# Query and key rows of a differential attention, split once over all 128 partitions

## The chip, the core and the metric

The kernel runs on one core of a Trainium2 chip. TensorE (PE) multiplies, VectorE (DVE) and ScalarE (ACT) read its results in PSUM and prepare operands in SBUF, GpSimd (POOL) does small work, and SyncE (SP) issues nearly all DMAs from one queue. Each engine runs its own queue in order. The metric is device time of one execution in microseconds (us), as the median of several runs; less is better.

## The reference

One layer: an RMS norm, one input projection, then two groups of heads side by side (differential attention, and a gated delta rule with a scan over chunks), an output projection, and an MLP with a squared ReLU. Everything is float32. The part that the change touches is the attention of group A, four heads with two softmax maps each:

```python
da_q = rms_norm(da_q.reshape(B, S, DA_HEADS, 2, DA_QK_DIM), q_norm_w[l])   # S = 1024, heads 4, dim 64
da_k = rms_norm(da_k.reshape(B, S, DA_HEADS, 2, DA_QK_DIM), k_norm_w[l])
...
s = jnp.einsum('bqhcd,bkhcd->bhcqk', qb, k) * scale
s = jnp.where(causal, s, jnp.finfo(jnp.float32).min)
p = jax.nn.softmax(s, axis=-1)
a = p[:, :, 0] - lam * p[:, :, 1]
out = jnp.einsum('bhqk,bkhe->bqhe', a, v)
```

## The kernel before

Float32 accuracy is made of products of rounded parts: an operand x becomes xH (rounded to the format that PE multiplies fast, `F32R`) and xL = x - xH. A large product is then three matmuls, H by H, H by L and L by H.

The work goes in stages. First come the projection of gates and of the delta rule's inputs (0 to about 250 us), then a stage in which many streams share PE (about 250 to 620 us), then the MLP. In the middle stage a planner, the class `Interleave`, writes PE's order: each stream is a generator that yields the time from which it can go on. The planner keeps its own clock `now`, which PE work advances (`flow.pe`). The streams have priorities: `scan` (the delta rule), `horner`, `mixed`, `da_turns`, `values`, `scores`, `da_units` and `outproj`. With `flow.chain` a stream estimates when a series of ACT and DVE instructions will be done, and with `flow.hold` how long a PSUM bank stays taken. The estimates are `act(n)` = 55 + 0.83 n ns and `vec(n, extra)` = 68 + 1.045 n + extra ns; `chain` adds a quarter of the series' length as margin (`MARGIN`). A store may be put off to a planned time (`flow.put_off`). PE's order is fixed this way; the order on ACT, DVE, POOL and SP is left to the framework's scheduler.

The streams around the change:

- `da_units` (L987) projects queries, keys and values in three units of 512 columns, eight blocks of 128 tokens each (matmuls L1012 to L1014, in two PSUM banks `pj`). Its weights come in pieces `wraw` (L211), which ACT rounds to `wH` (L213) and DVE subtracts to `wL` (L214).
- `leave` (L1028) empties a bank: ACT scales it to `qn` (L1040, or L1034 and L1035), POOL and DVE norm it. It queues the normed pieces of 256 columns (two heads of queries or of keys) in the list `late` and doesn't start while more than two stand there.
- `da_turns` (L957) takes each of the 32 pieces: PE transposes it into `ps_qkt` (L965, L966), so that a partition holds one of 2 x 64 components (m is the softmax map, 64 partitions each) and the columns are 2 heads x 128 tokens. ACT and DVE split it into a tile `qa` (L972, L973, two buffers), which goes to `qk_d` in DRAM (L977).
- `scores` (L1094) loads the keys of a head into `KS0` and `KS1`, one for each map (`load_head`, L1068), and for each block of 128 queries `qa` and `qb` (`load_q`, L1085 to L1087), one block ahead. A score is two matmuls over 128 partitions, `qa` by `KS` (L1148) and `qb` by `KS` (L1149): with H and L parts stacked in the two halves of the partitions, one gives HH + LL and the other LH + HL.
- `values` (L1175) transposes the weights of the softmax (L1189) and multiplies by the values (L1201); `outproj` (L1279) multiplies with the output weights (L1291 to L1293).

Before, `qa` was stored with the halves already in the place where the matmul wants them: for map 0 the H part in partitions 0 to 63 and L in 64 to 127, for map 1 the other way round. So a split took two ACT and two DVE instructions over 64 partitions each, DVE writing to the other half than it read. A key tile was loaded with one DMA, `qa` with one, and `qb`, its halves swapped, with two.

Of the kernel before, what the change touches and what calls it, by code (L numbers as in the profile page):

```python
# [9 lines left out]
F32 = mybir.dt.float32  # L10
F32R = mybir.dt.float32r
BF16 = mybir.dt.bfloat16
AF = mybir.ActivationFunctionType
ALU = mybir.AluOpType
# [4 lines left out]
P = 128  # L19
# [100 lines left out]
def act(n, accum=False):  # L120
    return "S", 55.0 + 0.83 * n + (93.0 if accum else 0.0)


def vec(n, extra=0.0):
    return "V", 68.0 + 1.045 * n + extra
# [7 lines left out]
def tile_hymba_layer(  # L133
# [6 lines left out]
    nc = tc.nc  # L140
    V, S, G, T = nc.vector, nc.scalar, nc.gpsimd, nc.tensor
# [49 lines left out]
    qk_d = dram.tile([2, 2, NT, P, 2, 2, P], F32, name="qk_d")  # L191
# [264 lines left out]
    for tb in range(NT):  # L456
        T.matmul(tail[:, 300 + 2 * tb:302 + 2 * tb], ssum_[:, tb * P:(tb + 1) * P], ones[:, 0:2],
                 start=True, stop=True)
# [305 lines left out]
    flow = Interleave()  # L764
# [3 lines left out]
    HF = (slice(0, 64), slice(64, 128))  # L768
# [186 lines left out]
    late, accs, vts, v_at, qa_free = [], {}, {}, {}, [0.0] * 3  # L955

    def da_turns():  # L957
        for i in range(4 * NT):
            while not late:
                yield flow.now + 50, None  # L960
            g, kind, tb, qn, t = late[0]
            r = yield from flow.bank("px", at=max(t + 2000, qa_free[i % 2] - 500))
            late.pop(0)
            pt = px.tile([P, 512], F32, tag="px", name="ps_qkt")
            T.transpose(pt[:, 0:P], qn[:, 0:P], ident)  # L965
            T.transpose(pt[:, P:2 * P], qn[:, P:2 * P], ident)  # L966
            flow.begun(("qa", i % 2))
            qa = sd.tile([P, 2, 256], F32R, tag="qa", name="qa", bufs=2)
            wv = qw if kind == 0 else kw
            for m in range(2):  # L970
                a, b = HF[m], HF[1 - m]
                S.activation(qa[a, m, :], pt[a, 0:256], AF.Copy, scale=wv[a])  # L972
                V.scalar_tensor_tensor(qa[b, m, :], pt[a, 0:256], wv[a], qa[a, m, :].bitcast(F32),  # L973
                                       ALU.mult, ALU.subtract)
            flow.pe(2 * TR)
            t = flow.chain(act(256), act(256), vec(256, 60), vec(256, 60), start=max(flow.now, qa_free[i % 2]))
            flow.put_off(t, ("qa", i % 2), lambda g=g, kind=kind, tb=tb, qa=qa: nc.sync.dma_start(  # L977
                qk_d[g, kind, tb], qa.bitcast(F32).rearrange("p m (h t) -> p m h t", h=2)))
            qa_free[i % 2] = t + DMA_T
            flow.hold(r, t)  # L980
            state["turned"] += 1
            if state["turned"] % (2 * NT) == 0:
                flow.due(lambda t, key: key[0] == "qa")
                state["da"] += 1
                state["da_t"] = flow.now + 6000
        sdctx.close()
# [77 lines left out]
    def load_head(h, pool):  # L1064
        KS = []
        for m in range(2):
            k = pool.tile([P, SEQ], F32R, tag=f"KS{m}", name=f"KS{m}")
            nc.sync.dma_start(k.bitcast(F32).rearrange("p (b t) -> p b t", t=P),  # L1068
                              qk_d[h // 2, 1, :, :, m, h % 2, :].rearrange("b p t -> p b t"))
            KS.append(k)  # L1070
        return KS

# [8 lines left out]
    def load_q(h, tb):  # L1081
        qa = ap.tile([P, 2, P], F32R, tag="qa", name="qa", bufs=2)
        qb = ap.tile([P, 2, P], F32R, tag="qb", name="qb", bufs=2)
        src = qk_d[h // 2, 0, tb, :, :, h % 2, :]
        nc.sync.dma_start(qa.bitcast(F32), src)  # L1085
        nc.sync.dma_start(qb[HF[0]].bitcast(F32), src[HF[1]])
        nc.sync.dma_start(qb[HF[1]].bitcast(F32), src[HF[0]])  # L1087
        return qa, qb

    order = [(0, t) for t in range(NT)] + [(1, t) for t in range(NT)]  # L1090
# [3 lines left out]
    def scores():  # L1094
        heads, loaded, npe, nsc, since = {}, {}, 0, 0, 0
        while state["da"] < 1:
            yield flow.now + 300, None
        heads[0] = load_head(0, ap), load_v(0, ap)
        q = load_q(*order[0])
        yield state["da_t"] + 3000, None  # L1100
        for u, (h, tb) in enumerate(order):
            if h == 1 and h not in heads:
                while not (state["scan"] and len(v_at) == NT):
                    yield flow.now + 300, None
                heads[1] = load_head(1, pools["a2"]), load_v(1, pools["a2"])
                loaded[1] = flow.now + 9000
            if h > 0 and state["da"] > 1 and 2 not in heads:
                heads[2] = load_head(2, ap), load_v(2, ap)
                loaded[2] = max(flow.now, state["da_t"]) + 4000
# [8 lines left out]
            if q is None and h > 0:  # L1118
                q = load_q(h, tb)
# [3 lines left out]
            if q is None:  # L1123
                q = load_q(h, tb)
                yield flow.now + 3000, None
# [381 lines left out]
    flow.add(2, values())  # L1507
    flow.add(3, scores())
    flow.add(1.6, da_turns())
    flow.add(4, da_units())  # L1510
    flow.add(1.4, mix_loads())
# [343 lines left out]
```

## Time and profile before

| | us |
|---|---|
| median of 3 runs | 1226.38 (1225.47 to 1226.53) |
| the profiled execution | 1226.58 |
| its span, first to last instruction | 1224.9 |
| PE busy in the span | 1212.0 |
| DVE busy | 850.0 |
| ACT busy | 604.6 |
| POOL busy | 121.0 |

The span is one execution under the profiler. Lines such as L972 are those of the listing above. A group of instructions is named by line, engine and operation, then output <- inputs, shapes and count. A wait is put down to whatever released it. PE is busy for almost the whole span, and its matmuls overlap in the records, so a busy share of 99% says only that there are few gaps. The granted clock is the share of its full speed at which PE was allowed to run.

### The profile page before, as it was taken

The page shows a single profiled execution, that of the slowest core. Times are in us where ns is not written, and L with a number is a line of the kernel's source. Part 1 is how long each engine was busy: PE and PEld are TensorE (multiplying, and loading weights), DVE is VectorE, ACT ScalarE, POOL GpSimd, SP SyncE. Part 2 cuts the span into 40 slices and gives each one's busy share as a digit, 9 for nine tenths or more (in the row PEclk, how much of TensorE's full clock was granted, in tenths as well). Part 3 has the DMA queues.
Part 4 walks back from the last instruction along what each step waited for, and adds up shares of the span by engine and source line. Part 5 has one row for each costly group of instructions (what it writes and reads, how often), then busy time and mean ns, then how long its engine had stood idle before and what let it go on. Part 6 is the DMA issues. An engine that isn't in the chain of part 4 may idle for free.

```text
span 1224.9 us, 17632 instructions
## 1 busy us (share of the span) xinstructions
PE 1212.0 (99%) x6330; PEld 1029.2 (84%) x6330; DVE 850.0 (69%) x1448; ACT 604.6 (49%) x1176; POOL 121.0 (10%) x162
## 2 busy tenths in 40 slices
PE   9999999999999999999999999999999999999998
PEld 9988888898888888888788888888888888888887
DVE  7786788477868577766798554566577955786553
ACT  8565545234556555656666444454554333333331
POOL 0011110223332230212100000000000000000000
PEclk9999999999999999999999999999999999999999
DMA  6564442456755584434528433443279855433301
GB/s 230 176 182 125 112 130 87 116 183 218 241 161 180 173 244 135 115 80 142 183 86 291 155 127 133 170 174 135 103 253 353 325 185 183 160 104 104 138 35 69
DMA packets 161087, 199.04 MB, mean 163 GB/s; under 512 B 21008, under 2 KB 120936, under 8 KB 161000
## 3 DMA queue, kind: packets, MB, share of 16 engines
q1 hardware_dynamic: 160856, 197.79, 49.3%
q8 instruction: 50, 0.82, 0.3%
q14 instruction: 37, 0.30, 0.1%
q10 hardware_dynamic: 144, 0.13, 0.0%
HBM read 132.32 MB, written 65.56 MB: 162 GB/s over the span
## 4 chain that ended last, share of the span: by engine, by line
PE 89%; DVE 4%; DMA 3%; ACT 2%; issue 1%; SPq 0%; POOL 0%; ACTq 0%; DVEq 0%
PE X L1454 5%; PE X L1453 5%; PE X L1452 5%; PE X L1768 4%; PE X L1769 4%; PE X L1770 4%; PE ps_dn L221 4%; PE ps_dn L219 4%; PE ps_dn L220 4%; PE ps_qk L1012 3%; PE Y L1454 3%; PE Y L1453 3%; PE Y L1452 3%; PE ps_qk L1014 3%; PE ps_qk L1013 2%; PE ps_o L1201 2%
## 5 line engine op out<-in xcount | busy, mean ns | idle before, releaser
L1371 ACT CAST hH<-ur 128x1024 fp32r<-128x1024 f32 x56 | 58.6, 1048 | 166.0 <-PE X L1769 79.7
L1372 DVE TENSOR_TENSOR hL<-ur,hH 128x1024 fp32r<-128x1024 f32 x56 | 68.5, 1224 | 79.8 <-ACT hH L1371 79.8
L1372 DVE TENSOR_TENSOR op<-raw,op 128x1024 fp32r<-128x1024 f32 x48 | 58.7, 1223 | 75.3 <-PE X L1453 42.3
L1768 PE MATMUL X<-hH 128*128 128x512 f32 x224 | 87.2, 389 | 0.0
L1769 PE MATMUL X<-hL,hH 128*128 128x512 f32 x224 | 87.2, 389 | 0.0
L1770 PE MATMUL X<-hH,hL 128*128 128x512 f32 x224 | 87.2, 389 | 0.0
L1012 PE MATMUL ps_qk<-wH,hH 128*128 128x512 f32 x192 | 82.2, 428 | 1.9 <-ACT qn L1040 1.9
L1014 PE MATMUL ps_qk<-wH,hL 128*128 128x512 f32 x192 | 75.8, 395 | 0.0
L219 PE MATMUL ps_dn<-hH,wH 128*128 128x512 f32 x192 | 75.7, 394 | 0.0
L220 PE MATMUL ps_dn<-hL,wH 128*128 128x512 f32 x192 | 75.6, 394 | 0.0
L1013 PE MATMUL ps_qk<-wL,hH 128*128 128x512 f32 x192 | 75.4, 393 | 0.1
L221 PE MATMUL ps_dn<-hH,wL 128*128 128x512 f32 x192 | 75.4, 393 | 0.0
L1372 DVE TENSOR_TENSOR hL<-dw,hH 128x1024 fp32r<-128x1024 f32 x56 | 68.2, 1220 | 3.2 <-ACT hH L1371 3.2
L1371 ACT CAST op<-raw 128x1024 fp32r<-128x1024 f32 x48 | 50.4, 1050 | 34.8 <-PE Y L1454 20.1
L1371 ACT CAST hH<-dw 128x1024 fp32r<-128x1024 f32 x56 | 58.6, 1047 | 16.7 <-DMA dw<-in_w_down_dram 5.1
L1157 ACT ACTIVATE pexp<-ps_sc,mx 128x128 f32<-128x128 f32 (+7 forms) x64 | 47.3, 740 | 26.1 <-DVE mx L1153 26.1
L595 DVE SCALAR_TENSOR_TENSOR cy<-cp,pv,cy 128x512 f32<-128x512 f32 x72 | 53.7, 750 | 7.8 <-ACT cy L593 7.0
L1153 DVE TENSOR_REDUCE mx<-ps_sc 128x1 f32<-128x128 f32 (+7 forms) x64 | 47.5, 754 | 14.1 <-PE ps_sc L1151 13.5
L1291 PE MATMUL ps_op<-wH,hH 128*128 128x512 f32 x128 | 53.6, 419 | 0.0
L1293 PE MATMUL ps_op<-wH,hL 128*128 128x512 f32 x128 | 50.3, 393 | 0.0
L1292 PE MATMUL ps_op<-wL,hH 128*128 128x512 f32 x128 | 50.0, 391 | 0.0
L1453 PE MATMUL Y<-hL,op 128*128 128x512 f32 x128 | 49.8, 389 | 0.0
(355 smaller groups left out, 3383.8 us busy)
## 6 DMA issues: line engine op xcount, KB each, us to landing
ur<-ud SPq DMA_DIRECT2D x28, 1024.0 KB, 4.9
raw<-in_w_up_dram SPq DMA_DIRECT2D x32, 512.0 KB, 3.7
dw<-in_w_down_dram SPq DMA_DIRECT2D x32, 512.0 KB, 7.2
qk_d<-qa SPq DMA_DIRECT2D x32, 256.0 KB, 3.1
ud<-ua SPq DMA_DIRECT2D x16, 512.0 KB, 4.0
ud<-s SPq DMA_DIRECT2D x16, 512.0 KB, 3.2
wraw<-in_w_in_dram SPq DMA_DIRECT2D x24, 256.0 KB, 3.5
wraw<-in_w_in_dram SPq DMA_DIRECT2D x48, 128.0 KB, 2.9
```

Of the source, the lines that this page charges most:

```text
L219: T.matmul(ps, lh(k), rh(k), start=(k == 0), stop=False)
L220: T.matmul(ps, lh(k), rl(k), start=False, stop=False)
L221: T.matmul(ps, ll(k), rh(k), start=False, stop=(k == n - 1))
L1012: T.matmul(ps, hH[:, 4 * kh + k, sl], wh[:, k, :], start=(kh + k == 0), stop=False)
L1013: T.matmul(ps, hH[:, 4 * kh + k, sl], wl[:, k, :], start=False, stop=False)
L1014: T.matmul(ps, hL[:, 4 * kh + k, sl], wh[:, k, :], start=False, stop=(kh + k == 4))
L1371: S.copy(dst[0], src)
L1372: V.tensor_tensor(dst[1], src, dst[0].bitcast(F32), ALU.subtract)
L1453: T.matmul(ps, op[0][:, k, cs], h[1][:, k, :], start=False, stop=False, skip_group_check=True)
L1768: T.matmul(o, v[0][:, j, sl], v[2][:, j, c], start=s0, stop=False, skip_group_check=True)
L1769: T.matmul(o, v[0][:, j, sl], v[3][:, j, c], start=False, stop=False, skip_group_check=True)
L1770: T.matmul(o, v[1][:, j, sl], v[2][:, j, c], start=False, stop=s1, skip_group_check=True)
```

## The change

A turned piece is split once over all 128 partitions: `qa[:, 0]` takes the H part and `qa[:, 1]` the L part of both maps, and the tile is stored as it lies. The halves are brought to their places when they are loaded: each key tile with two DMAs of 64 partitions, `qa` with two and `qb` with two. The planner's estimate for a piece changes with it, from two ACT and two DVE instructions to one of each.

```diff
-            for m in range(2):
-                a, b = HF[m], HF[1 - m]
-                S.activation(qa[a, m, :], pt[a, 0:256], AF.Copy, scale=wv[a])
-                V.scalar_tensor_tensor(qa[b, m, :], pt[a, 0:256], wv[a], qa[a, m, :].bitcast(F32),
-                                       ALU.mult, ALU.subtract)
+            S.activation(qa[:, 0, :], pt[:, 0:256], AF.Copy, scale=wv)
+            V.scalar_tensor_tensor(qa[:, 1, :], pt[:, 0:256], wv, qa[:, 0, :].bitcast(F32), ALU.mult, ALU.subtract)
             flow.pe(2 * TR)
-            t = flow.chain(act(256), act(256), vec(256, 60), vec(256, 60), start=max(flow.now, qa_free[i % 2]))
+            t = flow.chain(act(256), vec(256, 60), start=max(flow.now, qa_free[i % 2]))
             flow.put_off(t, ("qa", i % 2), lambda g=g, kind=kind, tb=tb, qa=qa: nc.sync.dma_start(
-                qk_d[g, kind, tb], qa.bitcast(F32).rearrange("p m (h t) -> p m h t", h=2)))
+                qk_d[g, kind, tb], qa.bitcast(F32).rearrange("p x (h t) -> p x h t", h=2)))
...
             k = pool.tile([P, SEQ], F32R, tag=f"KS{m}", name=f"KS{m}")
-            nc.sync.dma_start(k.bitcast(F32).rearrange("p (b t) -> p b t", t=P),
-                              qk_d[h // 2, 1, :, :, m, h % 2, :].rearrange("b p t -> p b t"))
+            kv = k.bitcast(F32).rearrange("p (b t) -> p b t", t=P)
+            for x in range(2):
+                nc.sync.dma_start(kv[HF[x]], qk_d[h // 2, 1, :, HF[m], x, h % 2, :].rearrange("b p t -> p b t"))
...
-        src = qk_d[h // 2, 0, tb, :, :, h % 2, :]
-        nc.sync.dma_start(qa.bitcast(F32), src)
-        nc.sync.dma_start(qb[HF[0]].bitcast(F32), src[HF[1]])
-        nc.sync.dma_start(qb[HF[1]].bitcast(F32), src[HF[0]])
+        parts = [qk_d[h // 2, 0, tb, :, x, h % 2, :].rearrange("(m r) t -> r m t", m=2) for x in range(2)]
+        for t, swap in ((qa, 0), (qb, 1)):
+            for x in range(2):
+                nc.sync.dma_start(t[HF[x]].bitcast(F32), parts[x ^ swap])
         return qa, qb
```

## The prediction

> **What bounds the kernel now.** I read the page first, then the busy time by stage, then what TensorE (PE) waited for, then the instructions around its longest wait, and last the chain that leads into that wait.
>
> ```profile
> span 1224.9 us, 17632 instructions
> PE 1212.0 (99%) x6330; PEld 1029.2 (84%) x6330; DVE 850.0 (69%) x1448; ACT 604.6 (49%) x1176; POOL 121.0 (10%) x162
> ...
> 260.00:300.00 40.00, 40.00 (x253) 35.49 (x252) 35.04 (x95) 18.94 (x51) 15.26 (x16) 1.00 0.68 216
> 300.00:335.00 35.00, 33.07 (x192) 28.59 (x191) 28.98 (x76) 15.67 (x42) 10.69 (x11) 0.95 0.75 235
> 335.00:400.00 65.00, 63.82 (x349) 53.77 (x348) 47.01 (x117) 41.97 (x113) 18.14 (x24) 1.00 0.58 177
> 400.00:460.00 60.00, 58.62 (x324) 50.22 (x322) 39.25 (x96) 34.39 (x85) 18.90 (x23) 1.00 0.70 210
> ```
>
> The first two rows are the page; the others are stretches of the span (length, then busy time of PE, PE's weight loads, DVE, ACT, POOL, then the granted PE clock, DMA share and GB/s). PE is idle for 1224.9 - 1212.0 = 12.9 us of the whole run, so a change that leaves PE's own instructions alone can win no more than that, plus time in which PE runs at a lower clock. The changed lines run between 261 and 455 us. There DVE is the second bound: 35.04 of 40 us at 260 to 300. The row to see is 300 to 335: PE loses 1.93 us and its clock is 0.95.
>
> The waits of PE from 250 to 575 us are these, all of them:
>
> ```profile
> PE ps_qk L1012 <- ACT qn L1040: 1.9, 1, 1.9
> PE ps_sc L1148 <- ACT pexp L1157: 1.4, 2, 0.9
> PE ps_at L1189 <- DVE pexp L1167: 1.0, 1, 1.0
> PE ps_at L1189 <- DVE hL L260: 0.6, 2, 0.4
> PE ps_at L1189 <- ACT om L1207: 0.6, 1, 0.6
> ```
>
> One wait of 1.9 us stands out: the projection (L1012) wants a PSUM bank that ACT has not yet emptied (L1040). PE's own order of time around it, and three stretches of 4 us:
>
> ```profile
> 306.49 0.39 PE L1014 MATMUL ps_qk<-wH,hL 128*128 128x512 f32 x1
> 308.79 0.50 PE L1012 MATMUL ps_qk<-wH,hH 128*128 128x512 f32 x1 [1.91 <-ACT qn L1040]
> ...
> 310.39 0.63 PE L1014 MATMUL ps_qk<-wH,hL 128*128 128x512 f32 x1
> ...
> 308.00:312.00 4.00, 3.21 (x12) 2.79 (x13) 3.84 (x9) 3.59 (x11) 2.23 (x2) 0.71 0.56 170
> 312.00:316.00 4.00, 4.00 (x21) 3.45 (x21) 3.93 (x13) 2.16 (x4) 2.45 (x3) 0.87 0.76 231
> ...
> 340.00:344.00 4.00, 3.05 (x20) 2.60 (x19) 3.47 (x12) 1.35 (x5) 2.11 (x3) 1.00 0.55 139
> ```
>
> After the gap the same L1014 takes 0.63 us in place of 0.39. The clock stands at 0.71 and 0.87 for two stretches, which loses (0.29 + 0.13) x 4 = 1.7 us. The gap of 0.95 us in 340 to 344 left the clock at 1.00. So the gap at 306.9 cost 1.9 + 1.7 = 3.6 us, and one half as long costs only its own length. The Trainium skill, page "TensorE: Matmul & The Clock Gate", Part 1, has the clock halve after at least one idle window of about 3.4 us. Here 1.91 us of idle were enough, so the measurement decides; by the rule alone the gap would be worth 1.9 us and the forecast below would come out 1.7 us higher.
>
> What led into the gap, by the chain of waits from 284 to 310 us:
>
> ```profile
> by line: DMA wraw<-in_w_in_dram 19.5%; DVE qa L973 11.2%; issue 10.7%; ACT osq L919 8.0%; DVE oc L914 5.4%; PE ps_qk L1012 4.4%; DVE S L881 4.3%; ACT qa L972 3.7%; DVE oc L924 3.5%; PE ps_o L912 3.4%; PE ps_A L852 3.4%; DVE sn L1052 2.8%; A
> ...
> 299.45 5.06 DMA wraw<-in_w_in_dram
> 304.59 0.63 ACT wH L213
> ...
> 306.30 0.48 DVE qa L973
> 306.81 0.70 DVE oc L914
> ...
> 308.05 0.70 ACT qn L1040
> ...
> 308.79 0.50 PE ps_qk L1012
> ```
>
> The chain runs through DVE (which frees the weight buffer late), a weight load of 5.06 us, ACT's rounding of it, then DVE and ACT again. The lines of the change hold 11.2% + 3.7% of these 26 us: 2.9 us of DVE and 1.0 us of ACT, 3.9 us together.
>
> **The change, part by part.**
>
> (1) Half of the splits go. Each of the 32 turned pieces now has one ACT and one DVE instruction over 128 partitions in place of two and two over 64.
>
> ```profile
> L973 DVE SCALAR_TENSOR_TENSOR qa<-ps_qkt,pv,qa 64x256 fp32r<-64x256 f32 x32 | 15.4, 483 | 7.5 <-ACT qa L972 6.6
> L972 ACT ACTIVATE qa<-ps_qkt,pv 64x256 fp32r<-64x256 f32 x32 | 15.0, 468 | 24.1 <-PE ps_qkt L966 12.9 <-DVE qa L973 7.6 <-DMA qk_d<-qa 2.8
> ...
> L595 DVE SCALAR_TENSOR_TENSOR cy<-cp,pv,cy 128x512 f32<-128x512 f32 x72 | 53.7, 750 | 7.8 <-ACT cy L593 7.0
> L924 DVE SCALAR_TENSOR_TENSOR oc<-oc,of,zgt 128x128 f32<-128x128 f32 x32 | 9.8, 368 | 0.2
> ...
> 344.09 0.37 ACT L1034 ACTIVATE vt<-ps_qk,rt 128x128 f32<-128x128 f32 x1 [0.78 <-PE ps_qk L1014]
> ...
> 344.80 0.58 ACT L1035 ACTIVATE qn<-ps_qk,rt 128x384 f32<-128x384 f32 x1
> ...
> ACT qa L972 <- DVE qa L973: 15.1, 16, 1.8
> DVE qa L973 <- ACT qa L972: 12.0, 16, 1.8
> ```
>
> Is one over 128 partitions as short as one over 64? The same DVE operation over 128 partitions takes 368 ns for 128 columns and 750 for 512: on a line between them 256 columns take 495, against 483 measured at 64 partitions. On ACT 0.37 and 0.58 give 0.475, against 0.468. So columns set the price, and the new ones cost what one old one cost. Removed: 32 x 483 = 15.4 us of DVE and 32 x 468 = 15.0 us of ACT. Nearly all of it lies beside PE's work and is worth nothing; what counts is the share on the chain into a gap. Before, the steps of a piece alternated ACT, DVE, ACT, DVE, and ACT, which runs its queue in order, stood 15.1 us waiting for DVE with other evictions behind it (last two rows: total, times, longest). That wait has no cause left. Into the gap at 306.9, half of 3.9 us falls away: 1.9 us, just the gap's length, before counting ACT's waits. I take the gap as gone (-1.9) or so short that the clock stays up (-1.7). Bounds: 0 (the 5.06 us load sets the end whatever DVE does) to -3.6.
>
> (2) The other waits of PE in the stage sum to 1.4 + 1.0 + 0.6 + 0.6 = 3.6 us. All hang on ACT or DVE, which are lighter until 455 us. Bounds 0 to -3.6; I take -1.0, nearer nothing, since the releasers (exponentials, hL, om) are not the changed instructions.
>
> (3) The planner that writes PE's order counts a turned piece shorter: its own formulas give 267.5 ns for the ACT and 395.5 for the DVE instruction, times 1.25 for its margin: 0.83 us. So the order of PE from 261 to about 570 us is drawn anew, and with it the waits. Before, 235 us (335 to 570) of such order held 3.6 us of waits; no row tells the new ones. Bounds -3.6 (covered in 2) to +6.6 (rival 2). I take +1.6, a little under half of what the old order held.
>
> (4) Transfers. Each load of a query piece has four DMAs in place of three, all of 64 partitions, and each key load of a head four in place of two. Bytes and run lengths stay.
>
> ```profile
> 559.57 0.59 SPq L1087 DMA_DIRECT2D qb<-qk_d  x1
> ...
> 564.30 0.30 PE L1148 MATMUL ps_sc<-KS,qa 128*128 128x128 f32 x1
> ...
> qa<-qk_d SPq DMA_DIRECT2D x32, 128.0 KB, 2.6
> qb<-qk_d SPq DMA_DIRECT2D x64, 64.0 KB, 2.8
> ...
> 329.13 1.00 SPq L1068 DMA_DIRECT2D KS<-qk_d  x2
> ...
> 333.64 0.31 PE L1148 MATMUL ps_sc<-KS,qa 128*128 128x128 f32 x1
> ...
> DMA to landing us min/median/max: 4.3/5.3/6.3
> ```
>
> An issue of 64 partitions occupies SP's queue for 0.59 us: 32 x 0.59 + 8 x 0.50 (two key loads took 1.00) = 23 us more of SP over some 300 us. Queued behind it are the weight loads, the scan's loads and the stores. The query loads are made one unit ahead. The last one is the tightest: issued at 559.57, landed 2.8 us later at 562.4, used at 564.30. Cover 1.9 us, against 0.6 us more. The chain above has none of them among its lines, so I count nothing there. The keys of the first head have less cover: issued at 329.13, used at 333.64, 4.5 us for a landing that takes at least 4.3 (last row, the key loads). A half more in front of it comes 0.5 us later. But the store that it waits for comes one ACT and one DVE step sooner (0.47 + 0.48 us). I take 0. Without that cover it costs 0.3 us (one issue against 0.2) up to 2.7 (rival 3). SP lateness elsewhere: 0 to 0.6 us for one place, taken as 0, since no wait of PE before names a transfer there.
>
> (5) The matmuls, their operands' sizes and the bytes stored do not change: 0.
>
> Sum: -1.9 - 1.7 - 1.0 + 1.6 + 0 = -3.0 us. The profiled execution took 1226.58 us around its span of 1224.9 (1.7 us outside it): 1223.6. The median of the three runs, 1226.38, lies 0.2 lower: **1223.4 us**. Own range of this case: 1219.2 (all of 1 and 2, nothing new: 1226.4 - 3.6 - 3.6) to 1223.9.
>
> **Rivals.**
>
> Rival 1, given back: the lighter engines do not move the time beyond 0.2% (2.45 us, about what a measurement of this kernel tells from no change). The 5.06 us load, among transfers that keep the DMA share at 0.75 in 300 to 335 us, holds the gap open, or it shrinks while the new order costs the same elsewhere. For it: PE is 99% busy and 15 us of other engines are mostly hidden. Against it: half of the changed lines on the chain equals the gap. Time 1226.4 (1224.0 to 1228.8).
>
> Rival 2, slower by the order: the planner lets a piece's two buffers turn sooner, 16 pieces of the first unit by 0.83 us each on two buffers, at most 16 x 0.83 / 2 = 6.6 us. The projection then comes earlier in PE's order, while the weight load and ACT's eviction come only 1.9 us sooner. The gap at L1012 becomes 1.9 + 6.6 - 1.9 = 6.6 us, 4.7 more than before, and the clock drops as before: 1231.1. It decides (over 2.45 us) once PE's lead exceeds 4.4 us. For it: pieces pace the projection in the plan. Against: PE has 40.00 of 40 us of work before the gap, and what is put later fills the time.
>
> Rival 3, the keys come late. The Trainium skill, page "DMA: Bandwidth & Descriptors", Rules for kernel authors, says that two transfers to disjoint halves of the partitions serialize, and advises one transfer of 128. As a mechanism here: each half lasts as long as the whole did, and the second follows. With 2.6 us (the 128 KB load) as the fixed part of 5.3, a second half adds 2.7 us. PE then waits about 2.7 us at 333.64; that gap is over 1.9, so the clock falls: 2.7 + 1.7 = 4.4 us. With the gains of (1) to (3): 1227.8; with the old gap kept too: 1230.8. For it: the cover of 0.2 us. Against: 64 KB on 64 partitions land in 2.8 us and 128 KB on 128 in 2.6, with no sign of the first of a pair holding up the second. By that rule, the trace does not decide, as no key load of 64 partitions is in it.
>
> **How the numbers follow.** Forecast 0.48, rival 1 0.23, rival 2 0.19, rival 3 0.10 (half within 0.2%, half above). Faster 0.48; same 0.23 + 0.05 = 0.28; slower 0.19 + 0.05 = 0.24. Range: from 1219.6, nearly all of the known waits gone, to 1230.0, where most of rivals 2 and 3 still lies within.
>
> **What would show it.** Right: L972 and L973 with 32 instructions each at about 470 and 480 ns over 128 partitions; ACT waiting for L973 no more; the clock at 1.00 from 300 to 335 us; no wait of 1.9 us at L1012; PE busy the same. Wrong: a PE gap over 1 us at another place with a clock under 1.00 behind it; a wait of L1148 for a key load; a per-instruction time of L972 or L973 well above the old one; weight loads that issue later behind the query loads.

## The result, and the profile after

| | before | after |
|---|---|---|
| median of 8 runs, us | 1225.98 (1225.47 to 1226.73) | 1230.47 (1228.07 to 1234.37) |
| ratio, 95% interval | | 1.0041 (1.0026 to 1.0056) |
| span of the profiled execution, us | 1224.9 | 1232.7 |

The changed kernel is 0.41% slower, about 5 us. The forecast was 1223.4 us, and its range ended at 1230.0: the sign was wrong, and the range missed by half a us. The profiled execution of after is its slowest run (1234.37 us at a mean clock of 0.997; the fastest of the eight took 1228.07 us at 0.999), so its trace may hold a bad stretch that a median run has not.

The page of after, its rows by stage (length, busy time of PE, weight loads, DVE, ACT, POOL, clock, DMA share, GB/s) and one stage of before that was not shown yet (the last row):

```profile
span 1232.7 us, 17614 instructions
PE 1213.4 (98%) x6330; PEld 1030.9 (84%) x6330; DVE 828.5 (67%) x1416; ACT 591.7 (48%) x1144; POOL 122.8 (10%) x162
...
300.00:335.00 35.00, 32.34 (x195) 27.69 (x194) 24.17 (x66) 15.75 (x45) 11.35 (x12) 1.00 0.79 224
335.00:400.00 65.00, 62.31 (x357) 53.55 (x356) 42.99 (x118) 37.94 (x106) 18.26 (x22) 1.00 0.56 158
400.00:460.00 60.00, 56.67 (x292) 46.82 (x292) 31.14 (x77) 26.50 (x63) 19.82 (x24) 1.00 0.70 207
460.00:520.00 60.00, 56.60 (x345) 50.61 (x344) 42.82 (x74) 34.80 (x79) 10.03 (x12) 0.95 0.50 132
```
```profile
460.00:520.00 60.00, 58.97 (x372) 52.49 (x371) 44.05 (x82) 35.47 (x84) 9.41 (x12) 1.00 0.42 123
```

DVE lost 21.5 us of busy time and ACT 12.9, and the clock from 300 to 335 us is back at 1.00. Yet PE now has 1232.7 - 1213.4 = 19.3 us without work in place of 12.9. Each of the four stages from 300 to 520 us lost time; before, only the first of them stood out.

The instructions of the new splits are half in number, and over 128 partitions each is as short as one of 64 was (groups by line and form; the second half of each group, 16 more with the key weights, has the same durations):

```profile
L971 DVE SCALAR_TENSOR_TENSOR qa<-ps_qkt,qw,qa 128x256 fp32r<-128x256 f32 x16 | 7.7, 481 | 8.5 <-ACT qa L970 8.4
L970 ACT ACTIVATE qa<-ps_qkt,qw 128x256 fp32r<-128x256 f32 x16 | 7.5, 473 | 15.5 <-PE ps_qkt L966 14.6 <-DMA qk_d<-qa 0.9
```

PE's waits from 250 to 575 us in after. (Its line numbers are smaller by two or three here: L1146 and L1147 are the scores, L1009 and L1010 the projection, L1199 the values.)

```profile
PE ps_sc L1147 <- DMA qb<-qk_d: 3.9, 4, 2.8
PE ps_o L1199 <- DVE qa L971: 2.1, 1, 2.1
PE ps_sc L1146 <- DMA KS<-qk_d: 1.8, 1, 1.8
PE ps_sc L1146 <- ACT pexp L1155: 1.3, 2, 0.9
PE ps_qk L1010 <- DVE wL L214: 0.8, 1, 0.8
PE ps_qk L1009 <- ACT qn L1037: 0.7, 1, 0.7
```

With four shorter rows they sum to 12.0 us; before it was 5.5. The difference is about the 6.4 us by which PE's idle time grew. The wait at the projection fell from 1.9 to 0.7, as forecast. But three waits stand first that did not exist before. Two are for transfers, `qb` 3.9 us and `KS` 1.8. The key loads are cut in two by the change; `qb` came in two halves before as well, but now it is issued behind a `qa` that is cut in two. The third, 2.1 us of L1199 behind a split, belongs to the new order: z3 and x5 below have it too (1.9 and 1.8 us), without any half loads of keys or `qa`.

The longest one, first on SP's queue (start, duration), then on PE, then the clock of PE in stretches of 4 us, and last what SP itself waited for most from 490 to 517 us (total, times, longest):

```profile
507.00 0.33 SPq L1216 DMA_DIRECT2D mixa_d<-om  x1
507.42 0.57 SPq L1085 DMA_DIRECT2D qa<-qk_d  x1
508.09 0.54 SPq L211 DMA_DIRECT2D wraw<-in_w_out_dram  x1
508.69 0.57 SPq L1085 DMA_DIRECT2D qa<-qk_d  x1
509.35 0.54 SPq L211 DMA_DIRECT2D wraw<-in_w_out_dram  x1
509.99 1.22 SPq L1085 DMA_DIRECT2D qb<-qk_d  x2
...
511.81 0.38 PE L1146 MATMUL ps_sc<-KS,qa 128*128 128x320 f32 x1
514.95 0.63 PE L1147 MATMUL ps_sc<-KS,qb 128*128 128x320 f32 x1 [2.75 <-DMA qb<-qk_d]
...
510.00:514.00 4.00, 2.20 (x13) 1.75 (x11) 1.70 (x4) 2.77 (x7) 2.15 (x3) 1.00 0.68 222
514.00:518.00 4.00, 3.05 (x10) 2.76 (x11) 2.25 (x4) 1.61 (x4) 0.86 (x1) 0.56 0.21 60
518.00:522.00 4.00, 4.00 (x21) 3.86 (x20) 1.80 (x5) 1.30 (x5) 0.30 (x1) 0.59 0.46 148
...
SPq L1216 <- DVE om L1210: 6.3, 2, 4.0
```

Before this, SP stood 4.0 us at the store of `om`, which waits for DVE. Then it issues without a pause from 507.0 to 511.2: two halves of `qa`, two weight loads between them, and last the halves of `qb`. The first matmul of the block (on `qa`) runs at 511.81; its partner wants `qb`, which lands 3 us later. The second half of `qa` accounts for only 0.66 us of this queue (508.69 to 509.35); the standing time and the two weight loads are the larger part. The wait costs 2.75 us and (0.44 + 0.41) x 4 = 3.4 us of clock.

### The profile page after: what moved, and what is told of

The parts are those of the page before. It is cut to its first block, busy times and chain, and to the rows that moved or that the text cites. A ratio compares the mean times of both kernels' runs of the same rounds, so it can differ in the third digit from the quotient of the medians.

```text
span 1232.7 us, 17614 instructions
## 1 busy us (share of the span) xinstructions
PE 1213.4 (98%) x6330; PEld 1030.9 (84%) x6330; DVE 828.5 (67%) x1416; ACT 591.7 (48%) x1144; POOL 122.8 (10%) x162
## 4 chain that ended last, share of the span: by engine, by line
PE 87%; DMA 5%; DVE 2%; issue 2%; ACT 2%; SPq 1%; POOL 1%; ACTq 0%; DVEq 0%; POOLq 0%
PE X L1451 5%; PE X L1452 5%; PE X L1450 5%; PE X L1766 4%; PE X L1768 4%; PE X L1767 4%; PE ps_dn L219 4%; PE ps_dn L221 4%; PE ps_dn L220 4%; PE Y L1451 3%; PE Y L1452 3%; PE ps_qk L1009 3%; PE Y L1450 2%; PE ps_qk L1010 2%; PE ps_qk L1011 2%; PE Z L1766 2%
## 5 line engine op out<-in xcount | busy, mean ns | idle before, releaser
L1009 PE MATMUL ps_qk<-wH,hH 128*128 128x512 f32 x192 | 80.8, 421 | 0.7 <-ACT qn L1037 0.7
L1010 PE MATMUL ps_qk<-wL,hH 128*128 128x512 f32 x192 | 75.1, 391 | 0.8 <-DVE wL L214 0.8
L213 ACT CAST wH<-wraw 128x512 fp32r<-128x512 f32 x64 | 37.3, 629 | 29.5 <-DMA wraw<-in_w_in_dram 16.0
```

The source lines that it names most:

```text
L1009: T.matmul(ps, hH[:, 4 * kh + k, sl], wh[:, k, :], start=(kh + k == 0), stop=False)
L1010: T.matmul(ps, hH[:, 4 * kh + k, sl], wl[:, k, :], start=False, stop=False)
```

## The experiments

18 kernels, in five groups on chips with their own runs of before beside them. All ratios are to before. Where an expectation speaks of "the order", it is the order in which the planner lays PE's work.

### Which part of the change costs: the order, the loads or the splits

x1: the whole change, but the planner's old estimate, so that PE's order is the one of before.

```diff
-            t = flow.chain(act(256), vec(256, 60), start=max(flow.now, qa_free[i % 2]))
+            t = flow.chain(act(256), act(256), vec(256, 60), vec(256, 60), start=max(flow.now, qa_free[i % 2]))
```


> The whole change, but the planner keeps the old estimate of two ACT and two DVE instructions a piece, so PE's order is that of before. Loads theory (the extra half-partition loads make queries and keys late): PE still waits for qb and KS, the time stays at 1228 to 1231 us. Order theory (the new order of PE is what costs): no such waits, and the lighter DVE closes the gap at 306.9 us, 1222 to 1224 us.

x2: before, with the new estimate alone (the reverse edit of that line).

> The kernel before with only the planner's estimate of a piece shortened to one ACT and one DVE instruction; splits, stores and loads as before. Loads theory: 1224.5 to 1227.5 us, no wait of PE for a query or key load. Order theory: 1229 us or more, with the gaps of the changed kernel at its places.

x3: before, with keys and `qa` loaded in halves. PE's order is that of before.

```diff
-            nc.sync.dma_start(k...., qk_d[h // 2, 1, :, :, m, h % 2, :]....)
+            for x in range(2):
+                nc.sync.dma_start(k....[HF[x]], qk_d[h // 2, 1, :, HF[x], m, h % 2, :]....)
...
-        nc.sync.dma_start(qa.bitcast(F32), src)
+        for x in range(2): nc.sync.dma_start(qa[HF[x]].bitcast(F32), src[HF[x]])
```


> The kernel before with its splits, its layout and its planner's estimate, but every key tile and every qa loaded in two halves of 64 partitions. Loads theory: 1229 us or more, PE waits of 1 to 3 us for qb or KS. Order theory: 1225.5 to 1226.5 us, the loads stay hidden as the prediction had it.

x4: splits once; the store puts the halves in place with two DMAs of 64 partitions; loads and estimate as before.

```diff
+            def store(g=g, kind=kind, tb=tb, qa=qa):
+                for m in range(2):
+                    nc.sync.dma_start(qk_d[g, kind, tb, :, m].rearrange("(x r) h t -> r x (h t)", x=2),
+                                      qa[HF[m]].bitcast(F32))
```


> Splits once over 128 partitions with the old estimate, but each piece is stored with two DMAs of 64 partitions that put the halves in place, so keys, qa and qb load as before. Loads theory and the prediction's first step: the gap at 306.9 us and its half clock go, 1222 to 1224 us, no PE wait for query or key loads. If the splits bring nothing: 1225.5 to 1226.5 us with the gap at 306.9 us still there. If two stores a piece cost as much as the loads did: 1228 us or more.

| | median us | ratio (95%) |
|---|---|---|
| before, same chip | 1225.44 | 1 |
| x1 whole change, old order | 1230.43 | 1.0043 (1.0030 to 1.0056) |
| x2 new estimate alone | 1233.09 | 1.0066 (1.0053 to 1.0078) |
| x3 half loads alone | 1230.52 | 1.0039 (1.0025 to 1.0053) |
| x4 split once, two stores | 1231.64 | 1.0051 (1.0039 to 1.0064) |

x1 shows that the new order is not needed for the loss. x3 shows that the half loads alone, with PE's order, the splits and the stores of before, cost as much as the whole change. In x3 the scheduler also moved some 20 of 1448 DVE and of 1176 ACT instructions (around 371 to 386, 454 to 461 and 505 to 509 us); what that costs is not separated. x2 and x4 cost too, each by another edit, so "the loads" was not yet the only cause. x4's loads are those of before, and yet PE waits 2.8 us for `qb` in it, and 3.2 us for the scan (L864); its additional issues are stores. x1 by stage and PE's waits of x1 (its lines are those of before), 250 to 575 us:

```profile
300.00:335.00 35.00, 35.00 (x215) 30.78 (x214) 26.11 (x71) 16.80 (x50) 11.38 (x12) 1.00 0.82 239
```
```profile
PE ps_sc L1149 <- DMA qb<-qk_d: 3.1, 2, 2.3
PE ps_sc L1148 <- ACT pexp L1157: 2.4, 2, 1.6
PE ps_at L1189 <- DVE hL L260: 1.1, 1, 1.1
PE ps_o L1201 <- ACT at L1191: 1.0, 1, 1.0
```

In the old order the gap at L1012 is gone altogether: PE is busy 35.00 of 35 us. What was won there comes back as 3.1 us of waits for `qb`, with a half clock of 1.7 us behind the longer one, and as 1.9 us more of the other waits. And x3, where nothing is won:

```profile
PE ps_qk L1012 <- ACT qn L1040: 1.7, 1, 1.7
...
PE ps_tr L250 <- DMA mt<-mixn_d: 1.2, 2, 0.8
PE ps_qk L1013 <- DVE wL L214: 1.0, 1, 1.0
PE ps_op L1291 <- ACT hH L259: 1.0, 1, 1.0
PE ps_sc L1149 <- DMA qb<-qk_d: 0.9, 1, 0.9
PE ps_sc L1148 <- DMA KS<-qk_d: 0.4, 1, 0.4
```

With six more rows these sum to 10.0 us against 5.5 before, and the span grew by 4.3 us. Only 0.4 us of it names a load that is cut here (`KS`), and 0.9 us one that is issued behind a cut one (`qb`). The rest are rows for a transposed input (`mt`), a weight piece (`wL` made from `wraw`) and operands behind it: work whose own DMAs go out on the same queue. That these are late because of the issues in front is an inference from the queue's order; only the total is shown. The row for `wL` doesn't speak for it: y5 below, which adds no load and costs nothing, has it as well (1.2 us).

### The same, each part by itself

z2: splits once, everything else as before. The halves then don't lie where the scores want them, so the scores mix wrong parts; instructions, bytes and DMAs are as timed. z3: z2 with the new estimate.

> The kernel before with the splits done once over 128 partitions, and nothing else: stores, loads and the planner's estimate stay, so the halves are not brought to their places and the scores mix the wrong parts. The work of PE, its order and all DMAs are those of before; ACT and DVE have 32 instructions less each. If the lighter engines gain what the prediction's first step says: the gap at 306.9 us and its half clock gone, 1221.5 to 1223.5 us. If ACT and DVE in a new order lose it elsewhere: 1226 to 1232 us; then the DMAs are not what made the splits with whole loads slow.

> As the run before, with the planner's estimate of the change, so with PE's order of the changed kernel and the DMAs of before; the scores mix the wrong parts. If the half loads are what costs in the changed kernel: 1224 to 1227 us. If its order of PE costs: 1228 us or more.

z4 is the first half of x3's diff (keys), z5 its second (`qa`).

> The kernel before with only the key tiles loaded in two halves of 64 partitions (8 DMAs more). Keys theory: PE waits 0.5 us or more for KS at the first head and the time rises by 1 to 3 us. Queries theory: 1225.5 to 1226.5 us.

> The kernel before with only the qa tiles loaded in two halves of 64 partitions (32 DMAs more, 18 us of the SP queue). Queries theory: most of the 4.8 us of both half loads together, 1228.5 to 1231 us, with PE waiting for qb and for weights behind it. Keys theory: 1225.5 to 1227 us.

| | median us | ratio (95%) |
|---|---|---|
| before, same chip | 1225.93 | 1 |
| z2 splits once | 1224.36 | 0.9991 (0.9981 to 1.0000) |
| z3 splits once, new order | 1226.44 | 1.0005 (0.9996 to 1.0014) |
| z4 keys in halves | 1226.85 | 1.0009 (1.0000 to 1.0017) |
| z5 `qa` in halves | 1228.41 | 1.0027 (1.0016 to 1.0038) |

The parts add up. Splits with the new order +0.05%, keys +0.09%, queries +0.27%: +0.41%, and after measured +0.41%. With the three intervals combined, the sum is known to about 0.2%, and the loads are priced in the order of before, so that it agrees to the last digit is luck. The two loads together, +0.36%, agree with x3 (+0.39%). The query halves are the largest single part, and the splits by themselves gain a little.

The closest pair is z3 and after: PE, DVE and POOL run the same instructions in the same order in both (four of ACT's stand elsewhere), and only the loads differ. After lies 0.36% above z3 (0.18 to 0.53, from the two ratios), 4.4 us. x1 and z2 are the same pair in the old order of PE, with some ten of DVE's and six of ACT's instructions moved; they differ by 0.52% (0.36 to 0.68). So the half loads cost in both orders, and in after they are most of the loss.

z2's stage from 300 to 335 us and its waits of PE from 250 to 575 us:

```profile
300.00:335.00 35.00, 34.88 (x213) 30.44 (x212) 26.28 (x72) 16.25 (x47) 10.62 (x12) 1.00 0.76 239
```
```profile
PE ps_sc L1148 <- ACT pexp L1157: 2.5, 2, 1.7
PE ps_at L1189 <- DVE hL L260: 1.1, 1, 1.1
PE ps_at L1189 <- DVE pexp L1167: 0.8, 1, 0.8
```

The gap and the clock's dip are gone, 3.6 us. The other waits, 3.6 us before, are now 5.3 (with two more rows of 0.5 and 0.4): 1.7 us come back where PE, ahead of its old time, waits for the exponentials and for `hL`. What is left is 1.9 us. The span of this execution, z2's fastest, is even 3.6 us shorter than the one of before; the medians, which decide, show 0.09%, 1.1 us (0 to 2.3).

### How much of it is the accident of an order

Two constants of the planner were nudged, which changes no instruction and only redraws the order: `HOP` from 180 to 190 (x8 on before, y1 on after, y4 on x5) and `MARGIN` from 0.25 to 0.26 (x7 on before, y2 on after, z1 on x5). x5 is x4 with the new estimate, and so the change without its half loads, but with two stores a piece.

> The changed kernel with its own planner estimate, but stored with two DMAs of 64 partitions a piece so that keys, qa and qb load as before (17 us more of the SP queue between 300 and 570 us than before, as in the run with the old estimate, not 26 to 29). If the half loads are the main cost: 1226 to 1228 us, with no wait for keys or queries over 0.5 us. If any extra load on the SP queue costs alike: 1229 us or more. If the new order of PE is the main cost: 1230 us or more, with gaps behind DVE and ACT.

> The kernel before with only the planner's margin at 0.26 in place of 0.25: no instruction more or less, but PE's order drawn anew. If a new order costs little (as the prediction had it, 1.6 us): 1225 to 1228 us. If the order of before is a lucky one and any other costs some 5 us: 1229 us or more.

> The kernel before with only the planner's step between engines at 190 ns in place of 180: a second order drawn anew, with the same work. If a new order costs little: 1225 to 1228 us. If the order of before is a lucky one: 1229 us or more.

> The changed kernel with the planner's step at 190 ns, the nudge with which the kernel before took 0.9993 of its time. If the change itself costs (its half loads): 0.3 to 0.5% above the kernel before again, 1229 to 1232 us, with waits for keys or queries. If only the draw of the order made it slow: anywhere from 1222 to 1233 us, and no lasting sign; below 1226 us would show a change that brings its 3 us in another order.

> The changed kernel with the planner's margin at 0.26, the nudge with which the kernel before took 1.0054 of its time. If the change itself costs some 4 us in any order: 1234 to 1237 us. If the order's draw is all: independent of the other pair, 1222 to 1233 us.

> Splits once over 128 partitions with the planner's estimate of the change, whole loads (two stores a piece), and the planner's step at 190 ns. If the splits gain and the half loads cost: below the changed kernel with that step by 2 to 5 us, 1222 to 1226 us. If the draw is all: no such order between the two.

> Splits once over 128 partitions with two stores a piece and whole loads, planner's estimate of the change and margin 0.26, the nudge with which the changed kernel took 0.9999 of the time before. If half loads cost in this order too: 1221 to 1224 us, under both kernels. If two stores cost as much as they save: 1224 to 1226 us.

| ratio to before (95%) | as it is | HOP 190 | MARGIN 0.26 |
|---|---|---|---|
| before | 1 | 0.9993 (0.9984 to 1.0001) | 1.0054 (1.0042 to 1.0066) |
| after | 1.0041 (1.0026 to 1.0056) | 1.0106 (1.0093 to 1.0119) | 0.9999 (0.9988 to 1.0009) |
| x5, whole loads | 1.0017 (1.0008 to 1.0026) | 1.0106 (1.0091 to 1.0120) | 1.0008 (0.9997 to 1.0019) |

The same work in another order spans 0.6% on before and 1.1% on after. After over before is +0.41% as drawn, +1.13% with HOP nudged and -0.55% with MARGIN nudged (quotients of the rows). So the sign of this change is not a property of the change alone. Whole loads against half loads with one and the same setting: 0.24% better, equal, 0.09% worse. These rows set half loads against whole loads with two stores a piece, 32 issues more, so they don't price the half loads alone; for the nudged orders no run does.

What an unlucky order looks like, PE's longest wait in y1 and the rows of time around it:

```profile
PE ps_tr L1382 <- DVE hL L257: 6.0, 1, 6.0
...
612.00:620.00 8.00, 4.91 (x16) 4.05 (x17) 4.02 (x7) 3.31 (x7) 0.00 (x0) 0.57 0.39 119
```

It lies at 609 to 615 us, where the middle stage passes into the MLP, 50 us after the last changed line, and x7 and y4 have it too (6.1 and 5.8 us). With the half clock behind it (0.43 x 8 = 3.4 us in that row) it costs about 9 us (before waits 1.1 us at this place); HOP 190 cost after 8 us and x5 11.

### The queue by itself

x6: after without the loads of `qb`; `qa` is used twice, so the LH and HL terms of the scores are left out. y5: before, with `qb` loaded ahead of `qa`. z6: before, with the first half of `qa` loaded a second time (32 more DMAs of 64 partitions).

```diff
-        nc.sync.dma_start(qa.bitcast(F32), src)
+        nc.sync.dma_start(qa.bitcast(F32), src); nc.sync.dma_start(qa[HF[0]].bitcast(F32), src[HF[0]])
```


> The changed kernel without the 64 loads of qb; the second score matmul uses qa again, so the cross terms of the split are left out of the scores. PE's order and work stay those of the changed kernel. If the SP queue is what costs (64 issues of 0.57 us, 37 us less): the waits for queries and keys go and the time falls by the 5.7 us that PE waited for them plus the half clock, to 1223 to 1226 us. If the order of PE is the cost: 1228 us or more, with gaps behind DVE and ACT.

> The kernel before with the two qb loads issued ahead of the qa load of the same block: the orders of PE, ACT, DVE and POOL are those of before, only the order of the SP queue differs. If SP's order has slack at these loads, as the prediction held: 1225 to 1227 us. If the SP queue is tight enough that any change of it delays keys or queries: 1228 us or more.

> The kernel before with the first half of qa loaded a second time behind the whole load, 32 DMAs more that bring the same values again. If the count of DMAs on the SP queue is what costs: 1228 to 1230 us as with half queries. If the half shape in place of the whole one costs: 1225.5 to 1226.5 us.

x6 took 1229.45 us, 1.0036 (1.0023 to 1.0050). The waits for `qb` went, but PE waited elsewhere, and next to nothing was won:

```profile
PE ps_qkt L965 <- ACT om L1204: 3.6, 1, 3.6
PE ps_o L1198 <- DVE qa L971: 1.9, 1, 1.9
```

This one speaks against the loads as the whole account: from the side of after, taking 64 loads away did not give back what adding 32 had cost before. y5 took 1226.15, 1.0004 (0.9995 to 1.0012): in before, which load stands first doesn't matter. z6 took 1238.7, 1.0105 (1.0092 to 1.0118), but not by the price of an issue. The second load writes where the first still writes, so SP stood and waited for the first to land, with all else behind it (SP's waits):

```profile
SPq L1085 <- DMA qa<-qk_d: 22.2, 27, 3.0
```

So 22 us in which SP stands blocked, in 27 pieces, and 32 more issues cost 13 us together. It does not tell the number of DMAs from their shape, which it was made for.

## Why the prediction was wrong

Step (1), the splits: right in its mechanism. One instruction over 128 partitions takes 473 and 481 ns (468 and 483 over 64); ACT no longer waits there for DVE's part of a split; the gap at the projection shrank to 0.7 us in after (1.5 in z3) and vanished in x1 and z2. But of the 3.6 us only the gap itself, 1.9, was there to win in most runs. The dip of the clock, 1.7 us, belonged to the execution that was profiled and to few others. In y5, whose PE, ACT, DVE and POOL run the order of before, the same gap left the clock at 1.00:

```profile
308.52 0.50 PE L1012 MATMUL ps_qk<-wH,hH 128*128 128x512 f32 x1 [1.94 <-ACT qn L1040]
...
308.00:312.00 4.00, 3.48 (x22) 3.04 (x22) 3.87 (x8) 3.35 (x10) 2.31 (x3) 1.00 0.55 169
312.00:316.00 4.00, 4.00 (x28) 3.61 (x27) 3.93 (x12) 2.29 (x5) 2.63 (x3) 1.00 0.75 236
```

A dip of 1.7 us takes 0.0014 from the mean clock, and 80 of the 100 executions of before beside the experiments have a mean of 1.000.

Step (2), the other waits, counted as -1.0: wrong in sign. In z2 they grew from 3.6 to 5.3 us, +1.7. PE that no longer stops at 307 us arrives sooner at its next operands, which were not made sooner. The upper bound of 0 was the error: a gap that closes uncovers what it had hidden.

Step (3), the new order, counted as +1.6: z3 against z2 is +0.14%, +1.7 us, the size taken. That is luck, for the new order has no price of its own: with the splits of before it costs 8.1 us (x2), under the whole change nothing (after against x1), and with two stores it gains 4 us (x5 against x4). Its bounds, -3.6 to +6.6, were narrower than what nudges of the planner did (-0.9 to +6.6 us on before, -5.2 to +8 us on after), and they were not carried into the chances: a step that can turn the sign alone left "faster" at 0.48. Rival 2, its mechanism, did not come about: the wait at the projection got shorter.

Step (4), the transfers, counted as 0: this is the step that failed. Its 23 us of extra SP time were nearly right. Between 300 and 570 us SP spent 124.5 us issuing 256 DMAs before, and 153.4 us on 290 after (sums over the trace). What was wrong was to price it at two places, the last query load and the first key load, and at nothing elsewhere because "no wait of PE before names a transfer there". A wait that is hidden is not named. And "the last one is the tightest" was a misreading: the trace of before has a tighter query load. The last `qb` half of one block is issued at 502.39 and used at 505.32, 2.9 us later, in place of the 4.7 us at the end; against a landing of 2.8 us that is a cover of 0.1 us, less than one more issue. At just this block PE waits for `qb` in x3 (0.88 us), x1 (0.79 us) and z5 (1.07 us):

```profile
502.39 0.59 SPq L1087 DMA_DIRECT2D qb<-qk_d  x1
...
505.32 0.34 PE L1149 MATMUL ps_sc<-KS,qb 128*128 128x384 f32 x1
...
509.63 0.41 PE L1149 MATMUL ps_sc<-KS,qb 128*128 128x384 f32 x1 [0.88 <-DMA qb<-qk_d]
```

The first two lines are of before, the third of x3. SP has no lack of time as a whole (in after it issues in 153.4 of the 270 us); in the runs with half loads it has just stood over 4 us at the store of `om` here and issues in a burst. In before's order the half loads alone cost +0.39% (x3), 4.8 us, of which the queries make three quarters (z5, 3.3 us) and the keys one quarter (z4, 1.1 us); in the new order they cost 4.4 us (after against z3).

Rival 3 was right in its place and small in its effect: PE does wait 1.8 us for the first keys in after. Its key loads (count, KB each, median us to landing):

```profile
KS<-qk_d SPq DMA_DIRECT2D x16, 256.0 KB, 5.2
```

A key load of half the size lands in 5.2 us; the whole took 5.3, so halving saved nothing (the trace tells the landing of only two of the eight whole loads and six of the sixteen halves). The Trainium skill, page "DMA: Bandwidth & Descriptors", Rules for kernel authors, has transfers to disjoint halves of the partitions serialize; this trace fits that and does not prove it. But z4 prices the halves of the keys at 0.09%, 1.1 us, not at the 4.4 of the rival: in z4 PE waits 0.2 us for them, and in after the clock stayed up behind the 1.8.

What stays open: whether the number of the DMAs or their half shape does it (z6 was to tell and did not); how much of it the moved ACT and DVE instructions are in x3 and z5; why two half stores (x4) cost 0.51% in the old order and 0.17% in the new one (x5); and why after without its `qb` loads is no faster. A cost of the queue that depends on the order would fit these, and is not shown.

## What to carry to other kernels

Price a DMA that is added to an in-order queue by what stands behind it on that queue over the whole stage, and not only by the place where its own bytes are due; cover that the trace doesn't name is still cover that can be used up. Take for every load the time from issue to first use, not only for the last one, and look hardest where the queue has just stood still. Take a dip of the clock in one trace as a price only when other executions have it too. Where a planner lays the order, test a change with the old order as well, and nudge the planner on both kernels before crediting or blaming an edit of less than about 1%. A saving on an engine that PE rarely waits for is worth the gap it closes, less what the next operands, unchanged, then make PE wait.

## What the runs showed of the hardware

A gap of PE does not always bring the half clock, nor by its length alone; even one and the same gap does it in one execution and not in another (1.91 us in before, 1.94 in y5). Nor is a short gap always free: in z4 two gaps of 0.62 and 0.91 us, 1.6 us from start to start, brought 3.4 us of half clock at 448 us; in before 0.49 and 0.89 us at the same place brought none. In before 1.91 us at 306.9 brought about 3.4 us of half clock; in after 2.75 us at 512.2 brought twice as much (about 6.8 us, from the rows above), while gaps of 1.83 us and 2.15 us left the clock at 1.00:

```profile
331.67 0.30 PE L1146 MATMUL ps_sc<-KS,qa 128*128 128x128 f32 x1 [1.83 <-DMA KS<-qk_d]
...
393.34 1.80 PE L1199 MATMUL ps_o<-vt,at 128*128 128x128 f32 x14 [2.15 <-DVE qa L971]
```

The two stages that hold them, 300 to 335 and 335 to 400 us, have 1.00 in their rows. An issue of 64 partitions holds SP as long as one of 128 (the median is 0.58 us for a half of `qa` in after and 0.54 us for a whole one in before), so cutting a load in two doubles its price on the queue. And a split of 256 columns takes as long over 128 partitions as over 64: 473 against 468 ns on ACT, 481 against 483 on DVE.
